# Neighbourhood probabilities turned by VectorE and by transfers inside SBUF

## The chip, the cores and the metric

The kernel runs on one core of a Trainium2 chip. The metric is the time of one execution on the device in microseconds (us). The core's engines are TensorE (PE in the profile; its weight loads are PEld), VectorE (DVE), ScalarE (ACT), GpSimd (POOL) and SyncE (SP), which here only issues transfers. They work from queues of their own and wait for each other through semaphores. SBUF and PSUM hold 128 partitions; TensorE writes PSUM only.

## The reference

Two layers of an encoder over 512 tokens of width 1024, in float32, batch 1, with a memory of 256 tokens:

```python
def hybrid_mixer(h, w_in, rpb, q_norm, k_norm, w_out, rows, cos, sin):
    proj = h @ w_in
    na_q, na_k, na_v, g_q, g_k, g_v = jnp.split(proj, IN_SPLIT_POINTS, axis=-1)
    na_out = neighbourhood_attention(na_q, na_k, na_v, rpb, rows)
    g_q = apply_axial_rope(rms_norm(g_q, q_norm), cos, sin)
    g_k = apply_axial_rope(rms_norm(g_k, k_norm), cos, sin)
    gqa_out = gqa_block_attention(g_q, g_k, g_v)
    return jnp.concatenate([na_out, gqa_out], axis=-1) @ w_out

for l in range(2):
    x = x + hybrid_mixer(rms_norm(x, norm_mix[l]), ...)
    x = x + memory_cross_attention(rms_norm(x, ...), rms_norm(mem, ...), ...)
    x = x + conv_ffn(rms_norm(x, norm_ffn[l]), ...)
return rms_norm(x, norm_final)
```

The neighbourhood attention has 8 heads of width 64. The tokens are a grid of 8 rows of 64, and a query sees a window of 8 rows by 16 columns, with a learned bias per head; outside the window the score is masked. Softmax runs over the window, and the output is the probabilities times the values.

## The kernel before

Activations are kept transposed: eight tiles of 128 features by 512 tokens. A float32 product is made of three matmuls in a reduced float type, from a high and a low part of each operand (`mm3`); weights are split into the two parts on the chip, ScalarE writing the high part (L269) and GpSimd or VectorE the low one (L270). A weight is loaded into one of two raw tiles by SyncE, ahead of its use.

The neighbourhood stage of a layer treats four head pairs p, each in two halves bp: a *unit* is u = 2p + bp, eight in a layer. A half is 256 queries, two blocks i of 128; each block sees 256 keys, two chunks c of 128. For each unit:

- `na_scores` (L743): 8 matmuls give the scores of 2 heads j by 2 blocks i in two PSUM buffers. VectorE adds the bias and takes the maximum (L762, 4 steps of 128x256), ScalarE takes the exponential with its sum (L768, 4 steps) into SBUF tiles named t.
- `na_normalise` (L772): VectorE inverts the sums (L774); GpSimd scales three of the four 128x256 blocks (L491), ScalarE one (L780).
- `na_transpose` (L783): TensorE turns the eight 128x128 blocks into PSUM (rows "tr<-ident,t"; like all operations of a plain engine wrapper they have line L63), and `split_psum` (L482) writes the high part by ScalarE (L484) and the low one by VectorE (L485).
- `na_values` (L799): 8 matmuls (rows "mm<-r,r") of the value blocks with the turned probabilities in two PSUM buffers; ScalarE (L814) and VectorE (L815, L816) add the parts.

`weave` (L161) writes TensorE's order: in stage s it takes each step for the unit s minus the step's offset, and at each `None` it lets a `Filler` put projection matmuls into the queue (neighbourhood and grouped-query projections), counted by a simple formula, until `NA_FILL` ns have been filled:

```python
weave(8, [(2, na_transpose), None, (1, na_normalise), (0, na_scores), None, (2, na_values), None],
      attn_fill.run, na_quanta)
```

So values and transposes of a unit come two stages behind its scores: 10 stages of three fills. TensorE and SyncE keep the order of the program; the order of VectorE, ScalarE and GpSimd is chosen by a planner at build time, with priorities set by `behind`. All wait for their operands in that order, so an instruction that waits holds what stands behind it on its engine.

Other things that the change passes on the queues: `split_k` (L682) writes a pair's keys for one half of the partitions, and `double` (L693) copies them to the other half by SyncE, later (`late(2, ...)`); pairs 2 and 3 of a layer need that copy before their scores. `straddle` (L729) builds the shifted value blocks by five transfers; `swap` (L870) exchanges rotary halves by four transfers of 64 KB for each grouped-query projection; `load_bias` (L615) and weight loads are on SyncE too. PSUM has four buffers "mm" for projections and value blocks, two "sc" for scores and two "tr".

Of the kernel before, what the change touches and what calls it, by code (L numbers as in the profile page):

```python
# [10 lines left out]
F32 = mybir.dt.float32  # L11
# [7 lines left out]
P = 128  # L19
S = 512  # L20
# [6 lines left out]
HD = 64  # L27
# [9 lines left out]
WIN = [0, 64, 192, 256]  # L37
# [6 lines left out]

GQA_ORDER = ["k", 0, 1, "v", 2, 3]

NA_FILL = 2550
GQA_FILL = [2300] * 16 + [4300, 3600, 3000, 3000]
MEM_FILL = [1, 1, 2, 2, 1, 3, 1, 3, 1, 3, 1]
N_ROWS = 3  # L50
# [110 lines left out]
def weave(n, steps, filler, quanta):  # L161


    last = max(st[0] for st in steps if st)
    for s in range(n + last):
        pieces = iter(quanta(s))
        for st in steps:
            if st is None:
                filler(next(pieces))
            elif 0 <= s - st[0] < n:  # L170
                st[1](s - st[0])
# [3 lines left out]
def encoder_kernel(ctx: ExitStack, tc: tile.TileContext, t: dict, out: bass.AP):  # L175
    nc = tc.nc
    PE, SP = Counted(tc, nc.tensor), InOrder(tc, nc.sync)
    late = Late(PE)
    ACT_IN_ORDER = InOrder(tc, nc.scalar)
    ACT, DVE, POOL = Free(nc.scalar), Free(nc.vector), Free(nc.gpsimd)  # L180
# [3 lines left out]
    wpool = ctx.enter_context(tc.tile_pool(name="wpool", bufs=N_W))  # L184
    rpool = ctx.enter_context(tc.tile_pool(name="rpool", bufs=21))
    tpool = ctx.enter_context(tc.tile_pool(name="tpool", bufs=14))
    spool = ctx.enter_context(tc.tile_pool(name="spool", bufs=24))
    psum = ctx.enter_context(tc.tile_pool(name="psum", bufs=2, space=PSUM))

    @contextmanager  # L190
    def behind(n):


        at = tc.cur_priority
        tc.cur_priority = at + n
        yield
        tc.cur_priority = at
# [3 lines left out]
    def nm(s):  # L201
        uid[0] += 1
        return f"{s}_{uid[0]}"

    def rtile(shape, dt=F32R):
        return rpool.tile([P, *shape], dt, tag="r", name=nm("r"), padded_shape=[P, *pad(shape)])
# [11 lines left out]

    def tmp(shape=(S,)):
        return tpool.tile([P, *shape], F32, tag="t", name=nm("t"))  # L220

    def small(n):
        return spool.tile([P, n], F32, tag="s", name=nm("s"), padded_shape=[P, 16])
# [4 lines left out]
    ps_mm = lambda: ps("mm", 4)  # L228
    ps_s = lambda: ps("sc", 2)
    ps_t = lambda: ps("tr", 2)  # L230
# [251 lines left out]
    def split_psum(hi, lo, ps, scale=None):  # L482
        if scale is None:
            ACT.copy(hi, ps)  # L484
            DVE.tensor_sub(lo, ps, f(hi))  # L485
        else:
            ACT.mul(hi, ps, scale)
            DVE.scalar_tensor_tensor(lo, ps, scale, f(hi), op0=ALU.mult, op1=ALU.subtract)
# [119 lines left out]
    for l in range(DEPTH):  # L608
# [131 lines left out]
        na = {}  # L740
# [28 lines left out]
                                       accum_out=sums[:, col])  # L769
            na[u] = es, sums  # L770

        def na_normalise(u):  # L772
            es, sums = na[u]
            DVE.reciprocal(sums, sums)  # L774
            for j in range(2):
                for i in range(2):
                    if i or j:
                        normalise(es[j][:, i, :], sums, 2 * j + i, POOL)
                    else:
                        ACT.activation(es[j][:, i, :], es[j][:, i, :], AF.Copy, scale=sums[:, 2 * j + i : 2 * j + i + 1])  # L780
            na[u] = es

        def na_transpose(u):  # L783
            es = na[u]
            pts = []
            for j in range(2):
                tr = ps_t()
                for i in range(2):
                    for c in range(2):
                        PE.transpose(tr[:, (2 * i + c) * P : (2 * i + c + 1) * P], es[j][:, i, c * P : (c + 1) * P], ident)  # L790
                pt = rtile((2, S))
                with behind(-20):
                    split_psum(pt[:, 0, :], pt[:, 1, :], tr)
                pts.append(pt)
            na[u] = pts

        o32s = {}

        def na_values(u):  # L799
            p, bp = divmod(u, 2)  # L800
            pts = na.pop(u)
            if bp == 0:
                o32s[p] = tmp()
            th = tmp((2, 2, P))
            o32 = o32s[p][:, 256 * bp : 256 * bp + 256].rearrange("p (i q) -> p i q", i=2)
            for j in range(2):
                po = ps_mm().rearrange("p (i n q) -> p i n q", i=2, n=2)
                for i in range(2):
                    b = 2 * bp + i
                    for c in range(2):  # L810
                        PE.matmul(po[:, i], vblk[p // 2][WIN[b] + P * c][:, 2 * (p % 2) + j, :],
                                  pts[j][:, :, (2 * i + c) * P : (2 * i + c + 1) * P], start=c == 0, stop=c == 1)
                r = slice(64 * j, 64 * j + 64)
                ACT.copy(th[r, :, 0], po[64:128, :, 0])  # L814
                DVE.tensor_add(th[r, :, 1], po[0:64, :, 1], th[r, :, 0])  # L815
                DVE.tensor_add(o32[r], po[0:64, :, 0], th[r, :, 1])  # L816
            if bp == 1:
                late(1, lambda: parts.__setitem__(p, split_out(o32s.pop(p))))
                bias[p] = None
                del qk["q", p], qk["k", p]  # L820
                if p % 2 == 1:
                    vblk[p // 2] = None

# [251 lines left out]
                gqa_eps()  # L1077
            return [NA_FILL] * 3

        weave(8, [(2, na_transpose), None, (1, na_normalise), (0, na_scores), None, (2, na_values), None], attn_fill.run, na_quanta)  # L1080
        weave(4 * NB, [(2, gqa_transpose_p), (1, gqa_normalise), (0, gqa_scores), (3, lambda u: gqa_values(u, 0)),
                       (4, lambda u: gqa_values(u, 1)), None], attn_fill.run, lambda s: [GQA_FILL[s]])
        attn_fill.finish()
# [330 lines left out]
```

## Time and profile before

| | |
|---|---|
| median of 3 runs | 1372.81 us (1372.71 to 1376.84) |
| profiled execution, span | 1373.2 us |
| its TensorE busy time | 1350.8 us, 98% |
| VectorE, ScalarE, GpSimd busy | 873.9, 676.8, 689.6 us |
| mean granted TensorE clock | 0.997 |

The profiled execution took its span of 1373.2 us, 0.4 above the median of the runs. In the profile an instruction's row has its start, its length, engine, line, operation, the tiles it writes and reads (out<-in), and in square brackets the idle time of its engine before it and what ended it. The neighbourhood stage of layer 0 lies from about 36 to 146 us and that of layer 1 from about 706 to 816 us.

### The profile page before, as it was taken

The page shows a single profiled execution, that of the slowest core. Times are in us where ns is not written, and L with a number is a line of the kernel's source. Part 1 is how long each engine was busy: PE and PEld are TensorE (multiplying, and loading weights), DVE is VectorE, ACT ScalarE, POOL GpSimd, SP SyncE. Part 2 cuts the span into 40 slices and gives each one's busy share as a digit, 9 for nine tenths or more (in the row PEclk, how much of TensorE's full clock was granted, in tenths as well). Part 3 has the DMA queues.
Part 4 walks back from the last instruction along what each step waited for, and adds up shares of the span by engine and source line. Part 5 has one row for each costly group of instructions (what it writes and reads, how often), then busy time and mean ns, then how long its engine had stood idle before and what let it go on. Part 6 is the DMA issues. An engine that isn't in the chain of part 4 may idle for free.

```text
span 1373.2 us, 19238 instructions
## 1 busy us (share of the span) xinstructions
PE 1350.8 (98%) x7068; PEld 1154.6 (84%) x7068; DVE 873.9 (64%) x1540; ACT 676.8 (49%) x1258; POOL 689.6 (50%) x493
## 2 busy tenths in 40 slices
PE   9999999999999999999999999999999999999997
PEld 7998799888888888888888978998788888888897
DVE  6676675565886188268546767745758833861874
ACT  6775676564543243233457657755554422432441
POOL 2566656626444443444544666657264444444441
PEclk9999999999999999999999999999999999999999
DMA  6763213222333332332265531133143333333331
GB/s 214 230 167 95 62 47 93 84 70 78 107 93 95 104 93 85 107 99 84 86 183 179 150 88 54 57 99 92 32 123 92 93 108 92 93 92 108 92 93 62
DMA packets 219358, 139.88 MB, mean 102 GB/s; under 512 B 6144, under 2 KB 212224, under 8 KB 219264
## 3 DMA queue, kind: packets, MB, share of 16 engines
q1 hardware_dynamic: 218160, 137.99, 34.2%
q8 instruction: 56, 0.92, 0.3%
q10 hardware_dynamic: 1104, 0.66, 0.2%
q14 instruction: 38, 0.31, 0.1%
HBM read 126.05 MB, written 2.10 MB: 93 GB/s over the span
## 4 chain that ended last, share of the span: by engine, by line
PE 90%; DVE 4%; ACT 2%; POOL 1%; DMA 1%; issue 1%; ACTq 0%; DVEq 0%; POOLq 0%
PE mm L76 80%; PE sc L76 6%; PE tr L63 3%; PE tr L76 1%; POOL lo L270 1%; DVE mm L428 1%; DVE xT L429 1%; DMA raw<-in_w_in 0%; ACT hi L269 0%; ACT t L768 0%; DVE r L705 0%; DVE s L924 0%; DVE xg L485 0%; DMA raw<-in_w_mem_q 0%; DVE t L815 0%
## 5 line engine op out<-in xcount | busy, mean ns | idle before, releaser
L270 POOL TENSOR_TENSOR lo<-raw,hi 128x1024 fp32r<-128x1024 f32 (+2 forms) x268 | 500.2, 1877 | 478.0 <-ACT hi L269 477.8
L76 PE MATMUL mm<-xg,hi 128*128 128x512 f32 x1920 | 595.6, 391 | 3.6 <-DVE t L816 2.1
L76 PEld LDWEIGHTS mm<-xg,hi 128*128 128x128 f32 x1920 | 356.3, 188 | 74.7 <-issue 2.3
L269 ACT CAST hi<-raw 128x512 fp32r<-128x512 f32 (+2 forms) x276 | 224.0, 835 | 329.4 <-PE mm L76 271.5
L76 PE MATMUL mm<-xg,lo 128*128 128x512 f32 x960 | 374.0, 390 | 0.0
L76 PE MATMUL mm<-r,hi 128*128 128x512 f32 (+1 forms) x1144 | 331.6, 374 | 2.0 <-DVE xg L442 1.6
L76 PEld LDWEIGHTS mm<-r,hi 128*128 128x128 f32 x1144 | 207.1, 189 | 40.3 <-DVE xg L442 3.3
L1238 DVE SCALAR_TENSOR_TENSOR t<-t,par,t 128x7 f32<-128x7 f32 (+1 forms) x352 | 201.9, 641 | 34.0 <-ACT t L1231 34.0
L76 PE MATMUL mm<-r,lo 128*128 128x512 f32 (+1 forms) x572 | 212.9, 372 | 0.0
L76 PEld LDWEIGHTS mm<-xg,lo 128*128 128x128 f32 x960 | 180.5, 188 | 38.2
L76 PEld LDWEIGHTS mm<-r,lo 128*128 128x128 f32 x572 | 107.8, 188 | 18.8
L1223 DVE TENSOR_TENSOR t<-mm,rep 128x512 f32<-128x512 f32 x88 | 60.1, 687 | 77.7 <-PE mm L76 62.1
L491 POOL TENSOR_SCALAR t<-t,s 128x512 f32<-128x512 f32 (+1 forms) x112 | 66.7, 610 | 72.9 <-DVE s L932 39.6
L1244 DVE TENSOR_TENSOR r<-t,r 128x512 fp32r<-128x512 f32 x44 | 90.4, 2056 | 7.4 <-ACT r L1243 4.3
L1240 ACT ACTIVATE t<-t 128x512 f32<-128x512 f32 x44 | 27.9, 633 | 134.7 <-DVE t L1238 134.6
L1267 DVE TENSOR_TENSOR xT<-xT,mm 128x512 f32<-128x512 f32 x32 | 21.9, 685 | 106.8 <-PE mm L76 106.8
L76 PE MATMUL sc<-r,r 128*128 128x256 f32 (+1 forms) x352 | 71.0, 334 | 1.7 <-ACT t L926 1.7
L1231 ACT ACTIVATE t<-t,par 128x512 f32<-128x512 f32 x88 | 66.8, 806 | 3.3 <-DVE t L1223 3.3
L63 PE MATMUL tr<-ident,t 128*128 128x128 f32 x456 | 63.1, 276 | 3.3 <-DVE s L932 1.2
L63 PEld LDWEIGHTS tr<-ident,t 128*128 128x128 f32 x456 | 53.1, 142 | 12.7 <-issue 5.8
L76 PE MATMUL mm<-r,r 128*128 128x256 f32 (+1 forms) x428 | 62.0, 297 | 0.6 <-DVE r L705 0.6
L76 PEld LDWEIGHTS mm<-r,r 128*128 128x128 f32 x428 | 56.2, 191 | 3.2 <-DVE r L705 0.8
(153 smaller groups left out, 1571.7 us busy)
## 6 DMA issues: line engine op xcount, KB each, us to landing
raw<-in_w_up SPq DMA_DIRECT2D x88, 512.0 KB, 3.7
raw<-in_w_in SPq DMA_DIRECT2D x33, 512.0 KB, 4.2
raw<-in_w_down SPq DMA_DIRECT2D x32, 448.0 KB, 3.6
raw<-in_w_mem_kv SPq DMA_DIRECT2D x16, 512.0 KB, 3.8
raw<-in_w_down SPq DMA_DIRECT2D x16, 512.0 KB, 3.9
r<-in_bias SPq DMA_DIRECT2D x16, 384.0 KB, 5.6
r<-r SPq DMA_DIRECT2D x22, 256.0 KB, 5.1
raw<-in_w_out SPq DMA_DIRECT2D x8, 512.0 KB, 3.6
```

The costliest lines, as they stand in the source:

```text
L63: return lambda *a, **k: self.tc.keep_in_program_order(op(*a, **k))
L76: return self.tc.keep_in_program_order(self.engine.matmul(out, lhsT, rhs, **k))
L269: act.copy(hi[:, k], raw[:, k])
L270: (POOL if eng[0] == "P" else DVE).tensor_sub(lo[:, k], raw[:, k], f(hi)[:, k])
L428: DVE.tensor_add(pm, pm, xT[c])
L491: eng.tensor_scalar(e, e, sums[:, col : col + 1], 1.0, op0=ALU.mult, op1=ALU.mult)
L1223: DVE.tensor_mul(u, us[side], ffn.rep)
L1231: ACT.activation(cc, u, AF.Identity, bias=par[:, l, CB + ch : CB + ch + 1], scale=w[1])
L1238: DVE.scalar_tensor_tensor(cc[:, dst], u[:, src], wi, cc[:, dst], op0=ALU.mult, op1=ALU.add)
L1240: ACT.activation(cs[0], cs[0], AF.Silu)
L1244: DVE.tensor_sub(acts[j][1], cs[0], f(acts[j][0]))
L1267: DVE.tensor_add(xT[m], xT[m], pm)
```

## The change

VectorE turns the probabilities in 32x32 blocks within each half pair: `na_turn` follows each normalised 128x256 block with a `DVE.transpose`, into a tile of 128x2048 for the whole head pair. Then `na_exchange`, once for each pair, moves 32-partition strips between the four partition groups by 16 transfers from SBUF to SBUF, all issued by SyncE, each of 32 partitions by 2 KB (64 KB), into a second tile of the same pool, which has two buffers. `na_split`, one stage later, writes the high parts by four ScalarE copies of 128x512 and the low parts by two VectorE and two GpSimd subtractions for the pair. `na_values_of` computes the values of both halves of a pair together, three stages behind the scores of the second half; its matmuls read the turned probabilities in runs of 32 columns. The weave has 11 stages with three fills of 2320 ns. The pool of small tiles has 23 buffers where it had 24, and the scratch for dynamic transfers is set to 1024 bytes.

```diff
@@ -44,7 +44,7 @@
 
 GQA_ORDER = ["k", 0, 1, "v", 2, 3]
 
-NA_FILL = 2550
+NA_FILL = 2320
 GQA_FILL = [2300] * 16 + [4300, 3600, 3000, 3000]
 MEM_FILL = [1, 1, 2, 2, 1, 3, 1, 3, 1, 3, 1]
 N_ROWS = 3
@@ -184,7 +184,8 @@
     wpool = ctx.enter_context(tc.tile_pool(name="wpool", bufs=N_W))
     rpool = ctx.enter_context(tc.tile_pool(name="rpool", bufs=21))
     tpool = ctx.enter_context(tc.tile_pool(name="tpool", bufs=14))
-    spool = ctx.enter_context(tc.tile_pool(name="spool", bufs=24))
+    spool = ctx.enter_context(tc.tile_pool(name="spool", bufs=23))
+    upool = ctx.enter_context(tc.tile_pool(name="upool", bufs=2))
     psum = ctx.enter_context(tc.tile_pool(name="psum", bufs=2, space=PSUM))
 
     @contextmanager
@@ -218,6 +219,9 @@
 
     def tmp(shape=(S,)):
         return tpool.tile([P, *shape], F32, tag="t", name=nm("t"))
+
+    def turned():
+        return upool.tile([P, 4 * S], F32, tag="u", name=nm("u"))
 
     def small(n):
         return spool.tile([P, n], F32, tag="s", name=nm("s"), padded_shape=[P, 16])
@@ -769,57 +773,86 @@
                                        accum_out=sums[:, col])
             na[u] = es, sums
 
-        def na_normalise(u):
-            es, sums = na[u]
+        turns, flats = {}, {}
+
+        def na_turn(u):
+
+            p, bp = divmod(u, 2)
+            es, sums = na.pop(u)
             DVE.reciprocal(sums, sums)
+            if bp == 0:
+                turns[p] = turned()
+            to = turns[p].rearrange("p (k j b q) -> p j b k q", k=8, j=2, b=4)
             for j in range(2):
                 for i in range(2):
                     if i or j:
                         normalise(es[j][:, i, :], sums, 2 * j + i, POOL)
                     else:
                         ACT.activation(es[j][:, i, :], es[j][:, i, :], AF.Copy, scale=sums[:, 2 * j + i : 2 * j + i + 1])
-            na[u] = es
-
-        def na_transpose(u):
-            es = na[u]
-            pts = []
+                for i in range(2):
+                    DVE.transpose(to[:, j, 2 * bp + i], es[j][:, i, :].rearrange("p (k q) -> p k q", q=32))
+
+        def exchange(src, chunks):
+
+            dst = turned()
+            to = dst.rearrange("p (r c n) -> p r c n", r=4, c=chunks)
+            of = src.rearrange("p (c r n) -> p r c n", r=4, c=chunks)
+            for d in range(4):
+                for q in range(4):
+                    r = (q + d) % 4
+                    SP.dma_start(to[32 * r : 32 * r + 32, q], of[32 * q : 32 * q + 32, r])
+            return dst
+
+        def na_exchange(u):
+            p, bp = divmod(u, 2)
+            if bp == 1:
+                flats[p] = exchange(turns.pop(p), 2)
+
+        def na_split(u):
+            p, bp = divmod(u, 2)
+            if bp == 0:
+                return
+
+            flat = flats.pop(p).rearrange("p (r c j h n) -> p c h r j n", r=4, c=2, j=2, h=2)
+            na[p] = [[rtile((2, 4, 2, HD)) for _ in range(2)] for _ in range(2)]
+            with behind(-20):
+                for h in range(2):
+                    for c in range(2):
+                        pt = na[p][h][c]
+                        ACT.copy(pt[:, 0], flat[:, c, h])
+                        (POOL if c else DVE).tensor_sub(pt[:, 1], flat[:, c, h], f(pt[:, 0]))
+
+        o32s = {}
+
+        def na_values(u):
+            p, h = divmod(u, 2)
+            pts = na[p][h]
+            if h == 0:
+                o32s[p] = tmp()
+            th = tmp((2, 2, P))
+            o32 = o32s[p][:, 256 * h : 256 * h + 256].rearrange("p (i q) -> p i q", i=2)
             for j in range(2):
-                tr = ps_t()
+                po = ps_mm().rearrange("p (i n r q) -> p i n r q", i=2, n=2, r=4)
                 for i in range(2):
                     for c in range(2):
-                        PE.transpose(tr[:, (2 * i + c) * P : (2 * i + c + 1) * P], es[j][:, i, c * P : (c + 1) * P], ident)
-                pt = rtile((2, S))
-                with behind(-20):
-                    split_psum(pt[:, 0, :], pt[:, 1, :], tr)
-                pts.append(pt)
-            na[u] = pts
-
-        o32s = {}
-
-        def na_values(u):
-            p, bp = divmod(u, 2)
-            pts = na.pop(u)
-            if bp == 0:
-                o32s[p] = tmp()
-            th = tmp((2, 2, P))
-            o32 = o32s[p][:, 256 * bp : 256 * bp + 256].rearrange("p (i q) -> p i q", i=2)
-            for j in range(2):
-                po = ps_mm().rearrange("p (i n q) -> p i n q", i=2, n=2)
-                for i in range(2):
-                    b = 2 * bp + i
-                    for c in range(2):
-                        PE.matmul(po[:, i], vblk[p // 2][WIN[b] + P * c][:, 2 * (p % 2) + j, :],
-                                  pts[j][:, :, (2 * i + c) * P : (2 * i + c + 1) * P], start=c == 0, stop=c == 1)
+                        PE.matmul(po[:, i], vblk[p // 2][WIN[2 * h + i] + P * c][:, 2 * (p % 2) + j, :],
+                                  pts[c][:, :, :, j, 32 * i : 32 * i + 32], start=c == 0, stop=c == 1)
+                po = po.rearrange("p i n r q -> p i n (r q)")
                 r = slice(64 * j, 64 * j + 64)
                 ACT.copy(th[r, :, 0], po[64:128, :, 0])
                 DVE.tensor_add(th[r, :, 1], po[0:64, :, 1], th[r, :, 0])
                 DVE.tensor_add(o32[r], po[0:64, :, 0], th[r, :, 1])
-            if bp == 1:
+            if h == 1:
                 late(1, lambda: parts.__setitem__(p, split_out(o32s.pop(p))))
                 bias[p] = None
-                del qk["q", p], qk["k", p]
+                del qk["q", p], qk["k", p], na[p]
                 if p % 2 == 1:
                     vblk[p // 2] = None
+
+        def na_values_of(u):
+            if u % 2 == 1:
+                na_values(u - 1)
+                na_values(u)
 
 
 
@@ -1077,7 +1110,8 @@
                 gqa_eps()
             return [NA_FILL] * 3
 
-        weave(8, [(2, na_transpose), None, (1, na_normalise), (0, na_scores), None, (2, na_values), None], attn_fill.run, na_quanta)
+        weave(8, [(2, na_exchange), (3, na_split), None, (1, na_turn), (0, na_scores), None, (3, na_values_of), None],
+              attn_fill.run, na_quanta)
         weave(4 * NB, [(2, gqa_transpose_p), (1, gqa_normalise), (0, gqa_scores), (3, lambda u: gqa_values(u, 0)),
                        (4, lambda u: gqa_values(u, 1)), None], attn_fill.run, lambda s: [GQA_FILL[s]])
         attn_fill.finish()
@@ -1403,7 +1437,8 @@
         arrays[n] = a[n]
     arrays = {f"in_{n}": np.ascontiguousarray(v) for n, v in arrays.items()}
 
-    nc = bacc.Bacc("TRN2", target_bir_lowering=False, num_devices=1)
+    nc = bacc.Bacc("TRN2", target_bir_lowering=False, num_devices=1,
+                   dynamic_dma_scratch_size=1024)
     t = {n[3:]: nc.dram_tensor(n, v.shape, mybir.dt.from_np(v.dtype), kind="ExternalInput").ap() for n, v in arrays.items()}
     out = nc.dram_tensor("out_0", (D, S), F32, kind="ExternalOutput").ap()
     with tile.TileContext(nc, schedule_with_timeline_sim=True) as tc:
```

## The prediction

> **What bounds the kernel now.** I read the page's busy shares first, then the chain of work that ended last, then the stretches in which the change works, then the rows of single instructions there.
>
> ```profile
> PE 1350.8 (98%) x7068; PEld 1154.6 (84%) x7068; DVE 873.9 (64%) x1540; ACT 676.8 (49%) x1258; POOL 689.6 (50%) x493
> PE 90%; DVE 4%; ACT 2%; POOL 1%; DMA 1%; issue 1%; ACTq 0%; DVEq 0%; POOLq 0%
> ```
>
> TensorE is busy for 98% of the span and is 90% of the chain that set the end. Work taken from its queue is time saved, and each stall put into the queue is time lost, microsecond for microsecond. The profiled execution spans 1373.2 us, 0.4 above the median of the three runs (1372.81), so I sum against the span and treat the two as one. 0.3% is about 4 us, which is what a measurement of this kernel can tell from no change.
>
> The neighbourhood stage of the two layers, in windows (start:end, length, then busy time of PE, PEld, DVE, ACT, POOL, the granted clock, DMA share, GB/s):
>
> ```profile
> 36.00:72.00 36.00, 36.00 (x221) 32.12 (x221) 24.82 (x64) 26.56 (x67) 22.17 (x23) 1.00 0.74 219
> 72.00:108.00 36.00, 35.56 (x248) 32.80 (x248) 24.02 (x64) 25.45 (x68) 20.32 (x24) 1.00 0.59 165
> 108.00:146.00 38.00, 35.54 (x208) 30.57 (x207) 27.01 (x57) 20.83 (x47) 25.82 (x25) 1.00 0.31 90
> 742.00:778.00 36.00, 36.00 (x247) 33.31 (x246) 26.00 (x71) 26.57 (x72) 19.49 (x21) 1.00 0.63 176
> 778.00:816.00 38.00, 35.85 (x199) 30.85 (x199) 24.99 (x51) 20.98 (x48) 24.70 (x25) 0.96 0.34 96
> 804.00:808.00 4.00, 4.00 (x16) 3.44 (x17) 1.33 (x3) 0.90 (x2) 1.89 (x3) 0.61 0.23 58
> ```
>
> TensorE is full there but for 0.44 + 2.46 us in layer 0 and 2.15 in layer 1. VectorE is at two thirds, so it can take work on average; whether it takes it in time is the question. The last row shows what a pause does: the clock averages 0.61 over 4 us. It follows this wait, the only one of its length in the stage:
>
> ```profile
> 800.71 1.05 PE L76 MATMUL mm<-ident,t 128*128 128x128 f32 x8
> 803.91 0.70 PE L76 MATMUL mm<-xg,hi 128*128 128x512 f32 x2 [2.15 <-DVE t L816]
> ```
>
> So that pause cost 2.15 plus 4 x 0.39 = 1.5 us. Layer 0's idle 2.9 and layer 1's 3.6, 6.5 us in all, are stalls of the old order, which the new one replaces by its own.
>
> **What is removed.** Eight TensorE transposes per unit (a unit is half a head pair), 16 units, 128 transposes:
>
> ```profile
> 38.81 1.12 PE L76 MATMUL sc<-r,r 128*128 128x256 f32 x8
> 39.85 0.39 PE L76 MATMUL mm<-hi,xg 128*128 128x256 f32 x1
> ...
> 53.51 1.03 PE L63 MATMUL tr<-ident,t 128*128 128x128 f32 x8
> 54.30 0.71 PE L76 MATMUL mm<-xg,hi 128*128 128x512 f32 x2
> 54.85 0.39 PE L76 MATMUL mm<-xg,lo 128*128 128x512 f32 x1
> 55.08 0.62 PE L76 MATMUL mm<-xg,hi 128*128 128x512 f32 x2
> 55.53 0.39 PE L76 MATMUL mm<-xg,lo 128*128 128x512 f32 x1
> 55.76 0.62 PE L76 MATMUL mm<-xg,hi 128*128 128x512 f32 x2
> ```
>
> From 53.51 to 54.30 is 0.79 us, and the pair of matmuls behind takes 0.55 to the next start instead of 0.45, so 0.88 a unit: 16 x 0.88 = **-14.0 us**. The three starts from 55.08 to 55.76 also give 0.68 us for three 512-column matmuls (2.72 for a fill of 12), and scores take 38.81 to 39.85, about 1 us.
>
> The evictions of the transposed blocks go too, and come back from SBUF. ScalarE's 32 copies at 0.59 us stay 32 copies; VectorE's 32 subtractions become 16 on VectorE and 16 on GpSimd:
>
> ```profile
> L485 DVE TENSOR_TENSOR r<-tr,r 128x512 fp32r<-128x512 f32 x50 | 33.3, 687 | 14.8 <-ACT r L484 14.4
> L484 ACT CAST r<-tr 128x512 fp32r<-128x512 f32 x50 | 28.2, 589 | 20.8 <-PE tr L63 20.2
> L513 POOL TENSOR_TENSOR r<-t,r 128x512 fp32r<-128x512 f32 x8 | 10.5, 1317 | 7.1 <-ACT r L512 4.1 <-PE mm L76 3.0
> L1244 DVE TENSOR_TENSOR r<-t,r 128x512 fp32r<-128x512 f32 x44 | 90.4, 2056 | 7.4 <-ACT r L1243 4.3
> L762 DVE CUSTOM_DVE_ANT_0 sc<-sc,r 128x256 f32<-128x256 f32 x64 | 25.4, 452 | 1.9 <-PE sc L76 1.9
> L491 DVE TENSOR_SCALAR t<-t,s 128x256 f32<-128x256 f32 x32 | 9.9, 351 | 0.3
> L705 DVE TENSOR_TENSOR r<-mm,r 64x512 fp32r<-64x512 f32 x28 | 19.3, 689 | 4.9 <-ACT r L703 4.4
> ```
>
> GpSimd gains 16 x 1.32 = 21 us, beside TensorE. VectorE's new subtraction has two SBUF inputs; its bounds are 0.69 (one input in PSUM) and 2.06 (the feed-forward's, SBUF inputs). I take 0.7, the nearest in size and place, and keep 2.06 for the range: 16 x 1.4 = +22 us of VectorE, of which perhaps half would lie on the path.
>
> **What is added.** (a) 64 VectorE turns of 128x256. No row shows one. The same tile costs 0.35 scaled and 0.45 read with a reduction; I take 0.4, so 8 turns of a head pair are 3.2 us. VectorE's total hardly moves: 64 x 0.4 + 16 x 0.7 - 32 x 0.69 = +15 us in two layers, where the first three windows alone leave it 110 - 76 = 34 us idle. On average it is hidden there; by order it is not (below).
>
> The Trainium skill (VectorE: DVE Perf Modes, The three transpose paths) gives 311 ns for a 128x128 bf16 block against 390 on TensorE; an estimate of two blocks by it is 0.62 us a turn, which no run here shows. By it a pair's turns take 5.0 us, 1.8 more, and with six pairs on the path the sum would be 1397.
>
> (b) 16 transfers of 64 KB per head pair on SyncE's queue, one issuing after another, 128 in all. The nearest are the rotary swaps, also 64 KB in SBUF from few partitions:
>
> ```profile
> 57.43 0.49 SPq L63 DMA_DIRECT2D r<-in_rope  x1
> 64.48 0.37 SPq L63 DMA_DIRECT2D raw<-in_w_in  x1
> 65.08 1.84 SPq L63 DMA_DIRECT2D r<-r  x2
> 100.30 2.47 SPq L63 DMA_DIRECT2D t<-t  x4
> t<-t SPq DMA_DIRECT2D x40, 64.0 KB, 2.0
> r<-r SPq DMA_DIRECT2D x16, 128.0 KB, 4.9
> ```
>
> Four issue in 2.4 to 2.5 us, 0.6 each, and land 2.0 after. An exchange is 16 x 0.6 + 2.0 = **11.6 us** (bounds: 0.37 an issue, as a weight load, gives 7.9; landing at 4.9 gives 14.5). Everything behind it on SyncE waits up to 9.6 us: weight loads (covered: their splits are used more than 25 us later), the key doubles, bias loads, straddles and swaps.
>
> (c) Four value blocks, two units, in one burst into the four PSUM buffers that the projections use as well. The moving operand now has runs of 32 columns. Runs of 128 cost nothing now (8 matmuls in 1.1 us, as the scores). I take zero; were it half as fast, 128 x 0.12 = +15.
>
> (d) The fill: 11 stages of 3 x 2320 ns for 10 of 3 x 2550, 76.6 against 76.5 us: nothing by itself.
>
> **Whether this is hidden.** Without values a stage is now 3 x 2.32 + 1 = 8 us. Scores of unit 0 stand at 38.81, so unit 4's are wanted near 70.5 and pair 0's values one score and one fill (1 + 2.9) later, near 74.4. On the other side: unit 1's probabilities are normalised as this shows, and the rotary load stands ahead of the exchange on SyncE:
>
> ```profile
> 54.04 0.18 DVE L774 RECIPROCAL s<-s 128x4 f32<-128x4 f32 x1 [0.99 <-ACT t L768]
> 54.32 2.33 POOL L491 TENSOR_SCALAR t<-t,s 128x256 f32<-128x256 f32 x3 [0.76 <-DVE s L774]
> ```
>
> Ready 56.7, turned 57.1, exchange 57.9 to 67.5, landed 69.5. Then:
>
> - The key doubles of pair 2, issued at 65.08 before, now stand behind the sixteen and a weight load: 68 to 69, landing 2 to 5 later, for scores wanted at 70.5. I take 74: a stall of **3.5**.
> - The next pair's turns need the first pair's tile, which is free at 69.5. VectorE's order puts all 8 (3.2 us) ahead of the subtractions, so these end near 74.2: just in time here.
> - VectorE then runs the key split (2 x 0.69), four bias steps (2.0) and a reciprocal before it frees the banks that the third and fourth value blocks wait for: about 81 against 79, another **2 to 3**.
> - Pair 1's exchange stands behind a memory load that waits for pair 0's value matmuls: it starts near 80, lands near 91.7, its values are wanted near 99, and the bank returns behind the turns, bias steps and rotary squares hold TensorE 1.5 and 2.4: **4**.
> - Pair 2 has its last unit normalised only near 117.5 and wants its values at 119.4; turns and subtractions are in between, and the third block waits for the first one's eviction: **4**. Pair 3 is wanted late: **1**.
>
> That is 15 us a layer. At least one of these pauses passes 2 us, as the one above, so 1.5 of clock: 16.5 a layer, 33 in two (layer 1 has the same order). Sum: 1373.2 - 14.0 - 6.5 + 33 = 1385.7, **1386 us**. Its own range, from stalls that are 2.5 us a layer shorter (1381) or 5 longer (1396), is 1380 to 1396.
>
> **The rivals.** *No new wait* (ends faster). If SyncE issues at 0.46 or less, pair 0's exchange lands by 67.3 and the doubles by 70.5, and later pairs gain as much: the deciding point is 16 issues in 7.4 us. For it: weight loads issue in 0.37. Against it: four swaps in 2.47. The stalls shrink to the last pairs' bank waits, 2 x 4: 1373.2 - 14.0 - 6.5 + 8 = 1361. Chance 0.24.
>
> *Balance*: stalls of about 10 a layer, if VectorE's order holds nothing: 1373.2 - 20.5 + 20 = 1373, within 4. Chance 0.12.
>
> *VectorE or the exchange sets the pace.* The loop of a pair is exchange 11.6, turns 3.2, subtractions 1.4 to 2.8, together 16 to 18 us, against 18.4 that TensorE needs for two stages with their values (2 x 8 + 2.4). With landings of 4.9, or subtractions of 2.06, it is 19 to 21 us: 2 to 3 more for each of six pairs and a clock loss for each of about four pauses, 1386 + 6 x 2 + 4 x 1.5 = 1404; half of it, 1395. Chance 0.15.
>
> *The DMA engines pace the exchange.* The first window moves 219 GB/s at a share of 0.74, so 296 when full, and leaves 77: the megabyte of pair 0 takes 13.6 us where SyncE issues it in 9.6. In the second window 115 GB/s are left, 9.1 us, which is hidden. So pair 0 alone is 4 us later in each layer: 1386 + 2 x 4 = 1394, and 1400 with a longer clock loss behind each. Chance 0.06.
>
> The Trainium skill (DMA: Bandwidth & Descriptors, Rules for kernel authors and Measured) speaks against the change here: it says to coalesce small transfers, and gives 0.95 us for one of 64 KB. Sixteen in a row by it are 15.2 us, 5.6 above the issue time, and on six pairs the sum by it would be 1420. The swaps' row, four in 2.47 us with landings 2.0 after, does not agree with that for transfers that overlap; no run here shows sixteen.
>
> **How the numbers follow.** The forecast has 0.43, the rivals 0.24, 0.12, 0.15 and 0.06. Slower is 0.43 + 0.15 + 0.06 = 0.64, same 0.12, faster 0.24. The range reaches down to the no-wait case at 1360, leaving out the half of that case that is faster still (0.12), and up to 1402, most of the way to the slow pace.
>
> **What would show it.** Right: PE stalls before scores of unit 4 with the key double as releaser, before the values with the new subtractions or evictions, exchanges of 9 to 10 us on SyncE's queue, turns near 0.4 us. Wrong: the neighbourhood stage of a layer ending earlier than 145 us, as the exchange issues faster, or turns over 0.6 us, which push VectorE's bias steps and with them the scores.

## The result, and the profile after

The changed kernel takes 1417.9 us in the median (1416.4 to 1421.3), where the kernel before took 1374.5 beside it: a ratio of 1.032, 95% interval 1.030 to 1.034, so some 43 us slower. The forecast was slower, 1386 us, and its range ended at 1402. The profiled execution after spans 1419.6 us, 46.4 more than the one before.

The page after, in its busy shares, its chain and two of its groups (busy us, mean ns | idle before, releaser):

```profile
PE 1359.4 (96%) x6940; PEld 1156.2 (81%) x6940; DVE 897.2 (63%) x1588; ACT 676.8 (48%) x1258; POOL 713.6 (50%) x509
PE 81%; DVE 6%; DMA 4%; ACT 2%; SPq 2%; POOL 2%; issue 2%; ACTq 0%; DVEq 0%; POOLq 0%
...
L76 PE MATMUL sc<-r,r 128*128 128x256 f32 (+1 forms) x352 | 76.7, 350 | 22.3 <-DMA r<-r 17.9
...
L76 PE MATMUL mm<-r,r 128*128 128x256 f32 (+1 forms) x428 | 65.5, 304 | 18.0 <-DVE t L844 8.6
```

TensorE has 128 instructions less and yet is busy 9 us longer, and its share of the chain fell from 90 to 81%. What grew in the chain are VectorE, transfers, GpSimd and the issuing queue (SPq). Two groups carry most of the waits: scores that wait for key copies (r<-r), and value matmuls that wait for evictions.

The stretches, with the columns as in the prediction, first after, then those of before that the prediction did not show:

```profile
36.00:72.00 36.00, 33.59 (x180) 28.84 (x179) 21.80 (x64) 23.37 (x64) 21.98 (x25) 0.95 0.76 211
72.00:108.00 36.00, 28.54 (x184) 26.06 (x182) 25.08 (x65) 19.88 (x52) 19.21 (x20) 0.91 0.69 186
108.00:146.00 38.00, 30.52 (x129) 25.18 (x130) 25.97 (x56) 18.32 (x45) 26.75 (x25) 0.73 0.47 121
146.00:176.00 30.00, 26.14 (x136) 21.80 (x135) 19.46 (x34) 16.92 (x36) 17.78 (x17) 0.94 0.38 110
...
742.00:778.00 36.00, 28.23 (x148) 24.21 (x147) 22.19 (x59) 19.13 (x49) 17.19 (x20) 0.90 0.76 213
778.00:816.00 38.00, 30.35 (x183) 27.12 (x182) 22.62 (x63) 21.54 (x58) 15.99 (x19) 0.87 0.47 124
816.00:866.00 50.00, 42.21 (x216) 35.51 (x215) 34.12 (x64) 24.41 (x53) 37.01 (x31) 0.93 0.51 133
```

```profile
146.00:176.00 30.00, 27.80 (x157) 23.16 (x156) 21.39 (x41) 19.46 (x45) 19.60 (x22) 1.00 0.21 62
...
816.00:866.00 50.00, 49.20 (x290) 42.35 (x289) 38.85 (x72) 35.35 (x80) 32.81 (x37) 1.00 0.19 51
```

Window length less busy time is TensorE's idle time: 21.2 us in layer 0 and 23.2 in layer 1, against 5.1 and 3.0 before, so 36 more. Busy time by one less the granted clock is an estimate of what half speed cost: 14 and 10 us, against 1.4 before, so 22 more. (TensorE's total says the same: 14 us of transposes less, and yet 8.6 us busier.) 36 + 22 less the 14 us of transposes is 44: nearly all of the 46.4 us lies in these two stretches, and of what they lose more than a third is clock.

The queue of SyncE shows the exchange (u<-u) and what stands behind it:

```profile
58.21 0.68 SPq L63 DMA_DIRECT2D r<-in_rope  x1
59.75 12.26 SPq L63 DMA_DIRECT2D u<-u  x16
72.13 0.52 SPq L63 DMA_DIRECT2D raw<-in_w_in  x1
72.75 1.19 SPq L63 DMA_DIRECT2D r<-r  x2
...
86.81 12.84 SPq L63 DMA_DIRECT2D u<-u  x16
...
111.76 10.24 SPq L63 DMA_DIRECT2D u<-u  x16
...
136.02 10.24 SPq L63 DMA_DIRECT2D u<-u  x16
```

And TensorE in layer 0, its waits before the scores of pair 2 (78.02 and 79.50) and at the values of pair 1:

```profile
78.02 0.77 PE L76 MATMUL sc<-r,r 128*128 128x256 f32 x2 [4.61 <-DMA r<-r]
79.50 1.62 PE L76 MATMUL sc<-r,r 128*128 128x256 f32 x6 [0.71 <-DMA r<-r]
...
106.28 1.20 PE L76 MATMUL mm<-r,r 128*128 128x256 f32 x8 [1.17 <-DVE r L823]
107.96 0.84 PE L76 MATMUL mm<-r,r 128*128 128x256 f32 x4 [0.49 <-DVE r L823]
111.25 1.22 PE L76 MATMUL mm<-r,r 128*128 128x256 f32 x4 [2.45 <-ACT t L901]
113.33 1.19 PE L76 MATMUL mm<-xg,hi 128*128 128x512 f32 x2 [0.85 <-DVE t L844]
```

The key copies of pair 2, issued at 65.08 before, go out at 72.75 behind the sixteen; the scores wait 5.3 us for them. At the values of pair 1 four waits follow each other, and the matmuls at 111.25 and 113.33 run at half the clock. Two more waits of layer 0, and its five spells of half clock:

```profile
62.12 0.51 PE L76 MATMUL sc<-r,r 128*128 128x256 f32 x2 [0.46 <-ACT t L772]
64.07 1.65 PE L76 MATMUL sc<-r,r 128*128 128x256 f32 x6 [1.45 <-ACT t L772]
```

```profile
64.03:67.44 3.41, 3.37 (x11) 2.99 (x12) 2.44 (x8) 2.05 (x4) 3.41 (x5) 0.50 0.47 110
77.68:84.51 6.83, 5.78 (x25) 5.54 (x26) 4.95 (x13) 2.50 (x10) 3.01 (x3) 0.50 0.96 286
108.40:118.64 10.24, 6.94 (x20) 5.21 (x19) 8.19 (x15) 6.09 (x17) 6.63 (x7) 0.50 0.63 159
135.71:145.95 10.24, 8.24 (x27) 7.00 (x28) 6.25 (x14) 3.79 (x8) 6.59 (x6) 0.50 0.45 102
169.84:173.25 3.41, 2.89 (x11) 2.70 (x12) 1.38 (x4) 2.47 (x6) 2.50 (x4) 0.50 0.51 154
```

Behind the two waits before 64 us the clock is back after 3.4 us. Behind a chain of pauses (the spell from 108.40) it stays at half for 10 us. The lengths are one, two and three times 3.41 us, and so it is in the traces of all the runs here: every spell of half clock, but for the one that each execution ends with, lasts one to four such steps (3.4, 6.8, 10.2 or 13.7 us). The falls go with TensorE's idle time within one step, in however many pieces: in the kernel before and the changed kernel the clock fell behind all ten steps at full clock in which it was idle for 1.66 us or more of the 3.41, and behind none with 1.40 or less (the ends of the executions left out). In the other traces both occur between 1.1 and 1.9 us. A further wait in a step at half (2.45 us in the first step from 108.40, 0.85 in the second) fits its staying low; but the spell from 135.71 went on for 7 us behind its last wait, and why is open.

VectorE's new rows, by form:

```profile
L793 DVE STREAM_TRANSPOSE u<-t 128x256 f32<-128x256 f32 x64 | 22.8, 413 | 7.8 <-DMA u<-u 6.3 <-POOL t L495 1.2 <-DMA t<-t 0.2
L823 DVE TENSOR_TENSOR r<-u,r 128x512 fp32r<-128x512 f32 x16 | 21.7, 1380 | 2.4 <-ACT r L822 2.4
L823 POOL TENSOR_TENSOR r<-u,r 128x512 fp32r<-128x512 f32 x16 | 21.6, 1366 | 11.2 <-ACT r L822 5.6 <-DMA t<-t 5.6
```

The turns take 0.41 us each. The subtraction with two inputs in SBUF takes 1.38 us on VectorE, between the bounds of 0.69 and 2.06.

### The profile page after: what moved, and what is told of

The parts are those of the page before. It is cut to its first block, busy times and chain, and to the rows that moved or that the text cites. A ratio compares the mean times of both kernels' runs of the same rounds, so it can differ in the third digit from the quotient of the medians.

```text
span 1419.6 us, 19227 instructions
## 1 busy us (share of the span) xinstructions
PE 1359.4 (96%) x6940; PEld 1156.2 (81%) x6940; DVE 897.2 (63%) x1588; ACT 676.8 (48%) x1258; POOL 713.6 (50%) x509
## 4 chain that ended last, share of the span: by engine, by line
PE 81%; DVE 6%; DMA 4%; ACT 2%; SPq 2%; POOL 2%; issue 2%; ACTq 0%; DVEq 0%; POOLq 0%
PE mm L76 73%; PE sc L76 5%; PE tr L63 2%; SPq L63 2%; PE tr L76 1%; POOL lo L274 1%; DMA r<-in_memT 1%; DMA r<-r 1%; DMA raw<-in_w_in 1%; DVE u L793 1%; DVE r L823 1%; DMA r<-in_rope 1%; DVE r L709 1%; DVE mm L432 1%; ACT hi L273 1%
## 5 line engine op out<-in xcount | busy, mean ns | idle before, releaser
L274 POOL TENSOR_TENSOR lo<-raw,hi 128x1024 fp32r<-128x1024 f32 (+2 forms) x268 | 501.3, 1882 | 459.0 <-ACT hi L273 458.9
L76 PE MATMUL mm<-xg,hi 128*128 128x512 f32 x1920 | 602.3, 395 | 0.9 <-DVE t L844 0.9
L76 PEld LDWEIGHTS mm<-xg,hi 128*128 128x128 f32 x1920 | 362.7, 191 | 74.8 <-ACT t L842 1.1
L76 PE MATMUL sc<-r,r 128*128 128x256 f32 (+1 forms) x352 | 76.7, 350 | 22.3 <-DMA r<-r 17.9
L76 PE MATMUL mm<-r,r 128*128 128x256 f32 (+1 forms) x428 | 65.5, 304 | 18.0 <-DVE t L844 8.6
L76 PEld LDWEIGHTS sc<-r,r 128*128 128x128 f32 x352 | 54.7, 203 | 30.4 <-issue 10.4
L959 ACT ACTIVATE t<-sc,s 128x512 f32<-128x512 f32 x64 | 44.1, 691 | 24.5 <-DVE s L957 21.7
```

Of the source, the lines that this page charges most:

```text
L76: return self.tc.keep_in_program_order(self.engine.matmul(out, lhsT, rhs, **k))
L274: (POOL if eng[0] == "P" else DVE).tensor_sub(lo[:, k], raw[:, k], f(hi)[:, k])
L959: ACT.activation(e, sc[j], AF.Exp, bias=nmx[:, c], accum_out=sums[:, c])
```

## The experiments

Ratios are against the kernel before on the same chip (1374.0 to 1374.9 us), with their 95% intervals.

**1. Without the transfers.**

```diff
-                flats[p] = exchange(turns.pop(p), 2)
+                flats[p] = turns.pop(p)
```

> The changed kernel without its 128 transfers: the split reads the tile that VectorE turned, so the strips are not exchanged between the partition groups and the output is not the reference's. Theory A (the exchange holds SyncE's queue for 12 us a pair, the key copies and memory loads behind it come late, TensorE stalls and then runs at half its clock): the waits for key copies go (17.9 us in the changed kernel) and with them most of the clock loss and the late values: 1370 to 1385 us. Theory B (VectorE's turns and the burst of four value blocks are what holds TensorE): at least 1400 us.

Measured 1399.3 us, 1.018 (1.016 to 1.020). The key copies are hardly waited for any more (1.3 us), as theory A has it, but 24.6 us remain, with theory B's waits:

```profile
PE mm L76 <- DVE t L844: 9.4, 7, 2.6
PE mm L76 <- ACT t L901: 3.8, 2, 3.1
PE sc L76 <- ACT t L772: 3.5, 3, 2.1
```

(us in total, times, longest.) So neither theory holds alone: transfers account for some 19 us, and something else for more than that.

**2. The kernel before, with the transfers alone.** A tile that nobody writes is copied by the same 16 transfers at the same place of SyncE's queue; TensorE still turns the probabilities. The pool of small tiles and the scratch have the changed kernel's sizes here, and the tile is cleared once at the start.

```diff
+                for d in range(4):
+                    for q in range(4):
+                        r = (q + d) % 4
+                        SP.dma_start(to[32 * r : 32 * r + 32, q], of[32 * q : 32 * q + 32, r])
...
-        weave(8, [(2, na_transpose), None, (1, na_normalise), (0, na_scores), None, (2, na_values), None], attn_fill.run, na_quanta)
+        weave(8, [(2, na_transfers), (2, na_transpose), None, (1, na_normalise), (0, na_scores), None, (2, na_values), None], attn_fill.run, na_quanta)
```

> The kernel before with TensorE's transposes, plus the same 16 transfers per head pair at the same place of SyncE's queue, from a tile that nobody writes any more into one that nobody reads: only SyncE's queue and the transfer engines are loaded. Theory A: the key copies come late in the old kernel too, with waits of 3 to 7 us before the scores of unit 4 in both layers and half clock behind them: 1390 to 1400 us. Theory B: nothing depends on the transfers, within 5 us of the kernel before.

Measured 1391.3 us, 1.011 (1.010 to 1.013), as theory A has it, though at another place:

```profile
57.15 13.89 SPq L63 DMA_DIRECT2D u<-still  x16
...
88.82 15.97 SPq L63 DMA_DIRECT2D u<-still  x16
104.89 0.54 SPq L63 DMA_DIRECT2D raw<-in_w_in  x1
105.54 3.19 SPq L63 DMA_DIRECT2D r<-r  x5
```

```profile
111.69 0.55 PE L76 MATMUL mm<-r,r 128*128 128x256 f32 x1 [5.55 <-DMA r<-r]
```

Here the scores of unit 4 hardly waited; the second exchange held back the five straddle transfers, and a value matmul waited 5.6 us for them. The 128 transfers that nobody reads, eight blocks of sixteen, cost 16 us.

**3. The key copies on another queue.**

```diff
-                    SP.dma_start(f(k[o]), f(k[r]))
+                    ACT.dma_start(f(k[o]), f(k[r]))
```

> The changed kernel with the key copies (two transfers a pair) issued from ScalarE's queue, so that they pass the exchange. Theory A: the 17.9 us of waits for them go, and some 6 us of half clock behind: 1390 to 1400 us. Rival: TensorE meets the next wait instead (values, evictions), and at most half of it is gained: 1405 us or more.

Measured 1411.6 us, 1.027 (1.025 to 1.028): 6 us gained of the 17.9 us of waits. The rival holds: TensorE met the next wait, the split of the exchanged tile.

```profile
PE mm L76 <- DVE r L823: 11.5, 5, 3.6
PE mm L76 <- ACT t L901: 6.8, 3, 3.1
PE mm L76 <- DVE t L844: 6.4, 6, 2.3
```

In the changed kernel L823 held TensorE for 2.4 us. Scores that no longer wait reach values that are not there yet.

**4. Work put into the pauses.**

```diff
+            n = {(0, 4): 18, (1, 4): 27, (1, 6): 17}.get((l, u), 0)
+            if n:
+                idle = ps_t()
+                for i in range(n):
+                    tc.keep_in_program_order(nc.tensor.matmul(idle, xg[0][0][:, 0:P], xg[0][0], start=i == 0, stop=i == n - 1))
```

> The changed kernel with 18, 27 and 17 extra 512-column matmuls (0.23 us each) whose result nobody reads, put on TensorE just ahead of the scores that wait longest for key copies (layer 0 unit 4, layer 1 units 4 and 6). They fill waits of 5.3, 7.8 and 4.8 us with 4.1, 6.1 and 3.9 us of work. If the pause costs only itself, the time is the same within 2 us; if the lower clock behind it costs as well, adding this work makes the kernel 4 to 8 us faster: 1410 to 1414 us.

Measured 1415.8 us, 1.030 (1.028 to 1.031). Fourteen microseconds of additional matmuls did not make the kernel slower, and the granted clock rose:

```profile
72.00:108.00 36.00, 30.94 (x199) 27.64 (x197) 25.93 (x71) 22.90 (x61) 21.80 (x21) 0.95 0.73 196
778.00:816.00 38.00, 33.63 (x206) 30.15 (x207) 24.16 (x65) 20.18 (x55) 18.72 (x19) 0.96 0.58 152
```

(0.91 and 0.87 without them.) The spells of half clock, without the last of the execution, sum to 34 us instead of 58, and the profiled span is 5.8 us shorter. The gain in the median, about 2 us, is less than the 4 expected and within the intervals of the two ratios, so that this run doesn't settle what the clock costs: like experiment 3, it lets TensorE arrive earlier at the next wait.

**5. Value halves apart.** The two halves of a pair have a fill between them, in the changed kernel and in it without transfers (the edit of experiment 1 beside it).

```diff
-(0, na_scores), None, (3, na_values_of), None]
+(0, na_scores), None, (3, lambda u: u % 2 and na_values(u - 1)), None, (3, lambda u: u % 2 and na_values(u))]
```

> The changed kernel with the value blocks of a head pair's two halves put apart by one fill (first half ahead of the third fill of the stage, second half behind it), all else the same. Theory C (four value blocks in one burst need all four PSUM buffers, and TensorE waits for evictions): of the waits for the evictions (VectorE L844 9.5 us, ScalarE L901 3.7 us) and the half clock behind them more than half goes: 1403 to 1412 us. Rival: the second half is early or late all the same because the exchange sets the pace: within 4 us of 1418.

> The same without the 128 transfers (the strips are not exchanged, so the output is not the reference's). Without transfers the changed kernel took 1399, of which 15.8 us are waits in or behind the bursts and about as much half clock. Theory C: 1372 to 1385 us. Rival (VectorE's turns and its two-operand subtractions delay the bias steps and the splits, wherever the values stand): 1392 us or more.

Measured 1411.4 us, 1.027 (1.025 to 1.029), and without transfers 1389.6, 1.011 (1.008 to 1.014). The burst costs 6 us in the one and 10 in the other: theory C in the first case, where the waits for the eviction L844 fell from 9.5 to 2.4 us, and only in direction in the second, where it asked for 14.

**6. Half of each exchange on ScalarE's queue.**

```diff
-                    SP.dma_start(to[32 * r : 32 * r + 32, q], of[32 * q : 32 * q + 32, r])
+                    (SP if d % 2 else ACT).dma_start(to[32 * r : 32 * r + 32, q], of[32 * q : 32 * q + 32, r])
```

> The changed kernel with half of each exchange issued from ScalarE's queue. Theory A: SyncE is held 6 us instead of 12.5, the key copies come 6 us earlier and the exchange lands earlier: 1395 to 1406 us. Rival: the transfer engines, not the issue, pace the megabyte, or ScalarE's issues delay its exponentials by as much: 1412 us or more.

Measured 1427.9 us, 1.039 (1.037 to 1.040): 10 us slower than the changed kernel, in the rival's range. ScalarE's half isn't issued in one piece but between its other work:

```profile
80.60 0.59 ACTq L803 DMA_DIRECT2D u<-u  x1
...
83.24 0.59 ACTq L803 DMA_DIRECT2D u<-u  x1
...
89.85 0.59 ACTq L803 DMA_DIRECT2D u<-u  x1
```

Eight issues spread over 10 us here. From its first issue to its last an exchange of layer 0 took 10.1, 16.1, 18.3 and 9.9 us: shorter than on one queue at the first pair, longer at the second and third, where SyncE's half began only behind ScalarE's. The key copies of pair 2 went at 73.89 all the same, behind a weight load, and the waits for key copies are 19.0 us in all, no less than the 17.9 with one queue. What makes the kernel 10 us slower was not taken apart.

**7. Longer pieces in the transfers.** The turned tile is laid out so that a transfer moves 32 rows of 2 KB, not 64 of 1 KB; VectorE writes 128x128 blocks for it.

```diff
-            to = turns[p].rearrange("p (k j b q) -> p j b k q", k=8, j=2, b=4)
+            to = turns[p].rearrange("p (r c j b q) -> p j b c r q", r=4, c=2, j=2, b=4)
...
-                    SP.dma_start(to[32 * r : 32 * r + 32, q], of[32 * q : 32 * q + 32, r])
+                    SP.dma_start(dst[32 * r : 32 * r + 32, 512 * q : 512 * q + 512], src[32 * q : 32 * q + 32, 512 * r : 512 * r + 512])
```

> The changed kernel with the turned tile laid out so that each 64 KB transfer is 32 rows of 2 KB instead of 64 of 1 KB (VectorE turns 128 blocks of 128x128 a pass in place of 64 of 128x256 for that). If the number of pieces paces the issue, an exchange issues in 10 us or less instead of 12.3 to 12.8 beside weight loads: 1408 to 1414 us. If SyncE's cost of a transfer or the full transfer engines pace it, the issue stays above 12 us and the time within 4 us of 1418, or above it by VectorE's extra turns.

Measured 1416.9 us, 1.030 (1.029 to 1.032): no difference. The first three rows of issues took 11.6, 11.8 and 10.0 us in layer 0, against 12.3, 12.8 and 10.2: neither the 10 us that the number of pieces would give, nor above 12. Half as many pieces are worth some 1 us at most. The long rows are those beside weight loads (transfer engines at a share of 0.76 and 0.69 in those windows), the short one beside a share of 0.47. The issues themselves, in the changed kernel (shortest, median, longest in ns):

```profile
L63 SPq DMA_DIRECT2D u<-u x128: 585/595/1606, 59.8 to 843.7; - x128
```

Nearly all take 0.6 us, beside weight loads too. The long rows have one to three pauses or long issues in them: in the first, 1.5 us between the seventh and the eighth transfer and 0.4 before the last; in the second, one issue and one gap of 1.6 us each. With longer pieces the pauses are there as well (1.3 us at the same place of the first row). What SyncE waits for in them is not shown.

**8. All subtractions on VectorE.**

```diff
-                        (POOL if c else DVE).tensor_sub(pt[:, 1], flat[:, c, h], f(pt[:, 0]))
+                        DVE.tensor_sub(pt[:, 1], flat[:, c, h], f(pt[:, 0]))
```

> The changed kernel with all four low parts of a pair subtracted on VectorE, none on GpSimd. Theory E (VectorE and GpSimd hinder each other on two-operand work in SBUF): a subtraction takes 0.7 us instead of 1.38 on VectorE, so its 32 cost what 16 cost now, GpSimd loses 24 us of work, and the time falls to 1408 to 1414. Rival: they stay above 1.2 us each (the operation costs that, or other GpSimd work is in the way), VectorE has 20 us more, and the kernel is 3 to 10 us slower.

Measured 1422.0 us, 1.034 (1.033 to 1.036): 4 us slower, as the rival has it, though a subtraction did get shorter (below its mean, then the shortest, median and longest in ns):

```profile
L823 DVE TENSOR_TENSOR r<-u,r 128x512 fp32r<-128x512 f32 x32 | 28.9, 949 | 1.3 <-ACT r L822 1.3
L823 DVE TENSOR_TENSOR r<-u,r x32: 649/685/1772, 77.1 to 850.6; 128x512 fp32r<-128x512 f32 x32
```

It takes 0.95 us instead of 1.38, so 0.43 us came from GpSimd's subtraction beside it. The trace tells where the rest stands: 23 of the 32 take 0.65 to 0.73 us, and 18 of these have nothing of GpSimd beside them; the other nine take 0.98 to 1.77, and each has GpSimd's low parts of weights (L274) or its step L922 beside it for two thirds of its time or more. So what is left goes with other work of GpSimd, which the rival named, and the operation alone costs the 0.7 us of theory E. The four in a row still end later than two beside two.

**9. The order alone.** The kernel before, with its TensorE transposes, in the changed kernel's order.

```diff
-NA_FILL = 2550
+NA_FILL = 2320
...
-(0, na_scores), None, (2, na_values), None]
+(0, na_scores), None, (3, lambda u: u % 2 and (na_values(u - 1), na_values(u))), None]
```

> The kernel before, TensorE transposes and PSUM evictions included, with the changed kernel's order only: values of both halves in one burst three stages behind the scores, 11 stages, fills of 2320 ns. Without transfers the changed kernel is still 24.6 us above before although it saves 14 us of TensorE. Theory C (the order does it: stages shorter than the softmax and bursts that wait for banks): 1385 to 1398 us. Theory D (VectorE's turns and two-operand subtractions do it): within 4 us of the kernel before.

Measured 1397.2 us, 1.017 (1.015 to 1.018). Theory C holds: with nothing turned on VectorE and nothing exchanged, the order costs 23 us. The largest wait is the bursts' own:

```profile
PE mm L76 <- DVE t L816: 8.2, 7, 1.9
PE mm L76 <- DVE r L705: 2.7, 2, 2.3
PE sc L76 <- ACT t L926: 2.4, 2, 2.1
```

L816 is the last eviction of a value block; in the kernel before it was waited for once. The grouped-query scores start at 154.6 us, where they started at 145.1.

**10. The order, with the halves apart.** The edit of experiment 5 in the kernel of experiment 9.

> The kernel before with the changed kernel's order, but the values of the two halves put apart by a fill. If the burst of four value blocks is most of what the order costs (22.8 us): 1378 to 1386 us. If the shorter stages and the later start of the grouped-query part are: 1391 us or more.

Measured 1386.1 us, 1.009 (1.007 to 1.011): half of the order's cost goes when the burst is parted. The other half is left to the shorter stages and the later grouped-query part; these two were not told apart.

**11. Order and transfers, nothing turned.** The edits of experiments 2 and 9 together.

> The kernel before with both the changed kernel's order (11 stages, fills of 2320 ns, bursts) and the 16 idle transfers per pair; TensorE still transposes. Alone the order cost 22.8 us and the transfers 16.5. If the two are independent causes: 1374.5 + 39 = 1414 us, and the turning itself (VectorE's turns and subtractions less 14 us of TensorE) would then be worth +4. If they are absorbed in the same waits: 1400 us or less, and the turning itself then costs 18 us or more.

Measured 1414.6 us, 1.030 (1.028 to 1.031). They add: 1.7% and 1.1% alone, 3.0% together. This leaves the turning itself, with VectorE's blocks and subtractions for TensorE's transposes, the step from 1.030 to 1.032: some 3 us, which the intervals do not tell from nothing. Experiments 1 and 9 say the same without transfers: 1399.3 us with the turning, 1397.2 with the order alone.

**12. Longer fills, and the parts that helped together.** Fills of 2600 ns without transfers and with the halves apart; then the full exchange with key copies on ScalarE's queue, the halves apart and fills of 2600 ns.

```diff
-NA_FILL = 2320
+NA_FILL = 2600
```

> The changed kernel without transfers (the output is not the reference's) and with the value halves apart, as measured at 1389.6, now with fills of 2600 ns instead of 2320, so that a stage is 8.8 us of TensorE work instead of 7.9. If short stages are what is left (scores wait for exponentials 3.1 us, then half clock): 1376 to 1384 us. If VectorE's queue is the bound: 1386 us or more.

> The changed kernel with key copies on ScalarE's queue, value halves apart and fills of 2600 ns: the three parts that helped or should help, together. If their gains add (6, 6 and 5 to 10): 1395 to 1402 us. If one loop of exchange, turns and subtractions sets the pace of a pair whatever TensorE does in between: 1405 us or more. It is not expected to beat the kernel before.

Measured 1390.4 us, 1.013 (1.010 to 1.015), no change from 1389.6; and 1409.2 us, 1.026 (1.024 to 1.027). Longer stages don't help. Without transfers the grouped-query scores start at 144.6 instead of 153.8 us, and the end is the same, probably because the projections that fill the stages are missing later. With all parts together the largest waits stand in the grouped-query part (the squares L901 ahead of its rotary step, and its exponentials L959):

```profile
PE tr L76 <- ACT t L901: 8.9, 4, 5.1
PE sc L76 <- ACT t L959: 6.9, 7, 2.1
```

The gains do not add. No version with the exchange came near the kernel before.

## Why the prediction was wrong

The direction and most places of the waits were right; two terms, the clock and the stalls, were too small, and one cause, the order, was put at nothing. The first bullets tell the missing time by kind, the one on fill and order by cause: order and transfers alone make up 40 us (experiment 11), and most of the stalls and of the clock loss below are theirs.

- *TensorE's saving of 14 us.* It fits the sum of the windows above, and it is used up: by experiment 11 the turning as a whole costs some 3 us, so that, if all 14 were saved, VectorE's and GpSimd's new work and the waits for it cost about 17.
- *Clock: 1.5 us a layer.* This is the step that failed by most. It measured 14 and 10 us. I counted one pause a layer, from one row of before. There were five spells of half clock in layer 0 and four in layer 1, and two of layer 0's lasted 10 us. 24 instead of 3 us is 21 of the 32 that the forecast missed.

The Trainium skill (TensorE: Matmul & The Clock Gate, Part 1) puts the fall to half rate behind an idle window of about 3.4 us and the return behind a busy one of the same length. The return agrees with the spell of 3.41 us from 64.03. The fall doesn't, if an idle window is one without work: TensorE was idle for 1.9 us in two pieces before 64.03, and for 1.7 in two pieces before 108.40, while waits of 1.4 and 1.5 us in the kernel before left it at 1.00.

- *Stalls of 15 us a layer.* Idle time is 21 and 23 us, 14 more than the 30 of the forecast; the old stalls that went were 9.5 us and not 6.5, which takes 3 back. By place: the wait for pair 2's keys was to be 3.5 and is 5.3 in layer 0 and 7.8 in layer 1, where pair 3's keys wait 4.8 more, which I had not counted. Pair 1's waits were to be 4 and are 5.0. Pairs 2 and 3 of layer 0 wait 4.2 and 1.0 at their values, for 4 and 1. Pair 0's bank waits were to be 2 to 3 and are 0.5, probably because the late scores had given VectorE time. Not foreseen were 1.9 us before 64 us, where scores wait for exponentials, and 2.9 at the first grouped-query scores.
- *The exchange at 0.6 us an issue.* The issue is right (median 0.595), the row of sixteen is not: 10.2 us where it runs through, and 12.3 to 12.8 with pauses in it, at the first two pairs of both layers, for 9.6. The landing of 2.0 us was right. The rival in which the transfer engines pace the exchange foresaw a longer row, with 4 us for pair 0 alone; that the engines make the pauses is not shown (experiment 7). The Trainium skill's 0.95 us for 64 KB (DMA: Bandwidth & Descriptors, Measured), from which the prediction worked out 1420, is for loads from HBM issued by GpSimd, another path than these transfers. The start of the second exchange behind a memory load was foreseen at 80 and is at 86.8.
- *Turns at 0.4 us.* Right (0.413). The 0.62 by the Trainium skill's block time (VectorE: DVE Perf Modes, The three transpose paths), which is one for bf16, is not what these turns take.
- *Subtractions at 0.7 us on VectorE.* It was 1.38, midway between the two rows. The operation alone takes 0.7; the excess stands where GpSimd works beside it, 0.43 of it with GpSimd's own subtractions (experiment 8). The row that I took as "the nearest in size and place" has an operand in PSUM; the one with both in SBUF was nearer in kind.
- *Fill and order: "nothing by itself".* This is the cause not seen. I compared the sums of the fills, 76.6 and 76.5 us, and took them as equal, and counted the burst's waits as a consequence of late probabilities. The order alone costs 23 us with probabilities that are early.
- *Value matmuls on runs of 32 columns at no cost.* Sixteen take 2.09 us at full clock, right.
- *The rival that ended faster* needed an issue of 0.46 us or less. The shortest exchange has 0.64. In the rival of the slow pace the sum is off: 19 to 21 us against 18.4 is 0.6 to 2.6 more a pair, not 2 to 3.

## What to carry to other kernels

Price a change of order on its own: put the new order on the old kernel and time that before the new operation is added. Count what stands behind a long block of issues in a queue, since eight blocks of sixteen transfers that nobody reads cost this kernel 16 us. On a kernel that TensorE bounds, price a run of short pauses by the clock as well as by their length; here half speed came to some 6 us for every 10 of new idle time.

## What was not expected of the hardware

The clock stays at half for whole steps of 3.41 us, one to four of them in the runs here, and waits of 1.2 and 0.5 us in one step were enough for a fall (before 108.40). The issue of a 64 KB transfer inside SBUF takes 0.6 us whether it has 32 pieces or 64; a row of sixteen takes 10.2 us, or up to 12.8 with pauses in it, and 15.97 in experiment 2. Transfers issued from ScalarE's queue went out between its instructions, eight of them over 10 us. A VectorE subtraction of two tiles in SBUF takes 0.7 us alone and up to 1.8 beside a GpSimd operation.
